# A gated product over rows: groups of four rows, two loads and one store a group, all on one DMA queue

## The chip, the core and the metric

The kernel runs on one core of a Trainium2 chip. The metric is the device time of one execution in microseconds (us). The engines that matter here are ScalarE (ACT), which computes the sigmoid, VectorE (DVE), which multiplies, SyncE (SP), which issues DMAs, and the core's 16 DMA engines, which move all data between memory (HBM) and the on-chip buffers of 128 partitions (SBUF). PE has no work, and GpSimd (POOL) only sets constants and clears semaphores.

## What is computed

```python
x = np.random.randn(8192, 8192).astype(np.float32)

def reference(x):
    a, b = np.split(x, 2, axis=-1)
    return a * (1 / (1 + np.exp(-b)))
```

Each row of x has 8192 numbers. The first half is multiplied by the sigmoid of the second half. 268.4 MB are read and 134.2 MB are written.

## The kernel before

**Tiles.** A tile is 256 rows: each of 128 partitions takes R = 2 adjacent rows, 64 KiB, which lie in one piece in memory. There are 32 tiles, `n_tiles`. The input buffers `xs` are two slots of 64 KiB a partition, and the output buffers `os` are two slots of 32 KiB a partition. Tile i uses slot i % 2 of both.

**One tile.** `load` (line 48) is one DMA of 8.4 MB on SP's queue, which appears in the profile as q1. `work` computes the sigmoid in place on ACT (line 61) and the product on DVE (line 72) into the packed output buffer. For most tiles this is one instruction of 128x8192 on each engine; the first and the last tile are worked in four pieces of 128x2048 (`fourths`). `store` (line 82) is one DMA of 4.2 MB, 32 KiB a partition, on ACT's queue, which appears as q10. Only the last tile is stored from SP's queue, in four parts of 1 MiB, each after its own product.

**What sets the order.** All waits are written by hand.
- A load waits at line 50 until the products of the tile two before it are done, because then its input slot is free. Loads 0 and 1 wait for nothing, and load 0 is moved ahead of the start-up barrier by `_launch_early`.
- The first sigmoid of a tile waits for its load (line 63).
- The first product of a tile waits on `ready` (line 65). This counts the sigmoid of this tile and the landing of the store two tiles earlier, which frees the output slot. Further pieces wait for their own sigmoid.
- A store waits for the products of its tile (line 83).

The queue of SP therefore holds the loads in order, and ACT's instruction stream alternates between a sigmoid and the issue of a store. `close` waits for everything and resets the semaphores.

Of the kernel before, what the change touches and what calls it, by code (L numbers as in the profile page):

```python
# [1 line left out]

# [4 lines left out]

P = 128
R = 2
SLOTS = 2  # L10


class _Program:

    def __init__(self, nc, x, out):
        self.nc = nc
        fp32 = mybir.dt.float32
        n_rows, n_cols = x.shape
        self.half = n_cols // 2  # L30
        self.n_tiles = n_rows // (P * R)
        self.x = x.rearrange("(n p r) m -> n p (r m)", p=P, r=R)
        self.out = out.rearrange("(n p r) m -> n p (r m)", p=P, r=R)
        self.xs = [nc.alloc_sbuf_tensor(f"x_sb{s}", [P, R * n_cols], fp32).ap() for s in range(SLOTS)]
        self.os = [nc.alloc_sbuf_tensor(f"o_sb{s}", [P, R * self.half], fp32).ap() for s in range(SLOTS)]
        self.loaded = [nc.alloc_semaphore(f"loaded{s}") for s in range(SLOTS)]
        self.ready = [nc.alloc_semaphore(f"ready{s}") for s in range(SLOTS)]
        self.product = nc.alloc_semaphore("product")
        self.sigmoid = nc.alloc_semaphore("sigmoid")
        self.arrived = nc.alloc_semaphore("arrived")  # L40
        self.last = nc.alloc_semaphore("last")
        self.to_ready = [0] * SLOTS
        self.products = self.sigmoids = self.lasts = 0
        self.done = {}

    def load(self, i, after=None):
        s = i % SLOTS
        ins = self.nc.sync.dma_start(out=self.xs[s][:, :], in_=self.x[i]).then_inc(self.loaded[s], 16)
        if i >= SLOTS:
            ins._wait_ge(self.product, self.done[i - SLOTS])  # L50
        return ins

    def work(self, i, pieces):

        nc, s = self.nc, i % SLOTS
        rows = self.xs[s].rearrange("p (r h m) -> p r h m", r=R, h=2)
        packed = self.os[s].rearrange("p (r m) -> p r m", r=R)
        waits = []
        for k, (r, c) in enumerate(pieces):
            b = rows[:, r, 1, c]  # L60
            sig = nc.scalar.activation(out=b, in_=b, func=mybir.ActivationFunctionType.Sigmoid)  # L61
            if k == 0:
                sig._wait_ge(self.loaded[s], 16 * (i // SLOTS + 1))
                self.to_ready[s] += 1 + (16 if i >= SLOTS else 0)
                waits.append((self.ready[s], self.to_ready[s]))
                sig.then_inc(self.ready[s], 1)
            else:
                self.sigmoids += 1
                waits.append((self.sigmoid, self.sigmoids))
                sig.then_inc(self.sigmoid, 1)  # L70
        for (r, c), wait in zip(pieces, waits):
            mul = nc.vector.tensor_mul(out=packed[:, r, c], in0=rows[:, r, 0, c], in1=rows[:, r, 1, c])  # L72
            mul._wait_ge(*wait)
            mul.then_inc(self.product, 1)
            self.products += 1
        self.done[i] = self.products

    def store(self, i, lo=0, hi=None, products=None):
        s, final = i % SLOTS, i == self.n_tiles - 1
        hi = R * self.half if hi is None else hi  # L80
        queue = self.nc.sync if final else self.nc.scalar
        ins = queue.dma_start(out=self.out[i][:, lo:hi], in_=self.os[s][:, lo:hi])
        ins._wait_ge(self.product, self.done[i] if products is None else products)
        if final:
            self.lasts += 16
            ins.then_inc(self.last, 16)
        else:
            ins.then_inc(self.ready[s], 16)
        return ins

    def trace(self):

        n, half = self.n_tiles, self.half
        whole = [(slice(0, R), slice(0, half))]
        fourths = [(slice(r, r + 1), slice(h * half // 2, (h + 1) * half // 2)) for r in range(R) for h in range(2)]
        self.load(1)
        for i in range(n):
            self.work(i, fourths if i in (0, n - 1) else whole)
            if i + SLOTS < n:
                self.load(i + SLOTS)  # L100
            if i < n - 1:
                self.store(i)
        for k in range(4):
            self.store(n - 1, k * half // 2, (k + 1) * half // 2, self.products - 3 + k)

    def close(self):


        nc, s = self.nc, (self.n_tiles - 2) % SLOTS
        for engine in (nc.scalar, nc.vector, nc.sync):  # L110
            engine.drain().then_inc(self.arrived, 1)  # L111
        nc.gpsimd.wait_ge(self.arrived, 3)
        nc.gpsimd.wait_ge(self.ready[s], self.to_ready[s] + 16)
        ids = sorted(h.num for h in (*self.loaded, *self.ready, self.product, self.sigmoid, self.arrived))
        assert ids == list(range(ids[0], ids[-1] + 1)) and self.last.num not in ids
        nc.gpsimd.sem_clear(range(ids[0], ids[-1] + 1))
        nc.gpsimd.drain()
        nc.sync.wait_ge(self.last, self.lasts).then_inc(self.last, -self.lasts)


def _launch_early(nc):

    SP = mybir.EngineType.SP
    entry, body = (b.instructions for b in nc.main_func.blocks[:2])
    load = next(i for i in body if i.engine == SP and i.opcode == "DMACopy")
    assert not load.sync_info.on_wait
    body.remove(load)
    where = next(k for k, i in enumerate(entry) if i.engine == SP and i.opcode == "Drain")  # L130
    entry.insert(where, load)


@with_exitstack
def kernel(
    ctx: ExitStack,
    tc: tile.TileContext,
    x: bass.AP,
    out: bass.AP,
):  # L140
    nc = tc.nc
    prog = _Program(nc, x, out)
    tc.info.no_tile_sem_insts.add(prog.load(0).ins.name)
    tc.close()
    tc.compile()  # L145
    _launch_early(nc)
    prog.trace()
    prog.close()


# [1 line left out]
_INS = ['x']  # L152
_OUTS = [((8192, 4096), 'float32')]


# [23 lines left out]
```

## Time and profile before

| what | value |
|---|---|
| median of 3 runs | 933.23 us (933.12 to 933.39) |
| the profiled execution | 933.08 us |
| its span | 931.8 us |
| DVE busy | 278.6 us (30%), 38 instructions |
| ACT busy | 226.8 us (24%), 39 instructions |
| moved over the span | 402.67 MB, 432 GB/s |
| q1, SP's queue | 5184 packets, 272.63 MB |
| q10, ACT's queue | 4464 packets, 130.03 MB |
| load, issue to landing | 42.2 us (median of 32) |
| store on ACT's queue, issue to landing | 34.8 us (median of 31) |

The span is the profiled part of the execution; the rest of its 933.08 us lies around it. A DMA is split into packets, and here a packet is the piece of one partition: 64 KiB of a load, 32 KiB of a store, 8 KiB of one of the four last stores. Each transfer also ends with 16 small packets of 4 bytes, one on each DMA engine, which raise the semaphore that others wait for. The share of a queue is the time that its packets took, against 16 engines' span.

### The profile page before, as it was taken

How to read it: one execution, taken by the hardware profiler on the slowest of the kernel's cores; microseconds unless marked ns; L12 is line 12 of the kernel's file. 1: busy time of each engine (PE TensorE's matmuls, PEld its weight loads, DVE VectorE, ACT ScalarE, POOL GpSimd, SP SyncE). 2: the span in 40 equal slices, each digit the busy share in tenths (PEclk: the TensorE clock that was granted, in tenths of full speed). 3: DMA queues.
4: the chain of work that ended last, by engine and by line, in shares of the span. 5: the costliest groups of instructions: out<-in, count | busy, mean ns of one | idle time of the engine just before them, and what ended most of it. 6: DMA issues, size and time to landing. Idle time of an engine off the chain costs nothing.

```text
span 931.8 us, 190 instructions
## 1 busy us (share of the span) xinstructions
DVE 278.6 (30%) x38; ACT 226.8 (24%) x39; POOL 0.2 (0%) x4
## 2 busy tenths in 40 slices
DVE  0333213333133331233312333123331233312333
ACT  1323330233311333113331133311333203332033
POOL 0000000000000000000000000000000000000000
DMA  9999999999999999999999999999999999999999
GB/s 405 428 450 428 422 456 405 450 428 428 450 421 435 428 436 442 428 428 450 450 405 430 442 456 428 412 463 408 450 428 428 450 408 447 428 428 450 426 429 405
DMA packets 9649, 402.67 MB, mean 432 GB/s; under 512 B 1072, under 2 KB 1072, under 8 KB 1072
## 3 DMA queue, kind: packets, MB, share of 16 engines
q1 hardware_dynamic: 5184, 272.63, 67.7%
q10 hardware_dynamic: 4464, 130.03, 32.3%
q14 instruction: 1, 0.01, 0.0%
HBM read 268.44 MB, written 134.22 MB: 432 GB/s over the span
## 4 chain that ended last, share of the span: by engine, by line
DMA 73%; DVE 15%; ACT 12%; DVEq 0%; issue 0%
DMA x_sb<-in_x_dram 73%; DVE o_sb L72 15%; ACT x_sb L61 12%; DVEq L111 0%
## 5 line engine op out<-in xcount | busy, mean ns | idle before, releaser
L72 DVE TENSOR_TENSOR o_sb<-x_sb 128x8192 f32<-128x8192 f32 (+1 forms) x38 | 278.6, 7344 | 647.1 <-ACT x_sb L61 647.1
L61 ACT ACTIVATE x_sb<-x_sb 128x8192 f32<-128x8192 f32 (+1 forms) x38 | 225.5, 5949 | 693.9 <-DMA x_sb<-in_x_dram 693.9
L61 ACT ACT_TABLE_LOAD x1 | 1.3, 1283 | 1.4 <-PEq L145 1.4
L163 POOL MEMSET const-bfloat16-1.0<- 128x1 bf16 x1 | 0.1, 102 | 0.0
L163 POOL MEMSET const-uint8-127<- 128x1 uint8 x1 | 0.1, 102 | 0.0
L163 POOL MEMSET const-float32-0.0<- 128x1 f32 x1 | 0.1, 99 | 0.2 <-issue 0.2
L163 POOL MEMSET const-float32-1.0<- 128x1 f32 x1 | 0.1, 99 | 0.0
## 6 DMA issues: line engine op xcount, KB each, us to landing
out_dram<-o_sb ACTq DMA_DIRECT2D x31, 4096.0 KB, 34.8
out_dram<-o_sb SPq DMA_DIRECT2D x4, 1024.0 KB, 5.7
x_sb<-in_x_dram SPq DMA_DIRECT2D x32, 42.2
```

What stands on the lines that cost most here:

```text
L61: sig = nc.scalar.activation(out=b, in_=b, func=mybir.ActivationFunctionType.Sigmoid)
L72: mul = nc.vector.tensor_mul(out=packed[:, r, c], in0=rows[:, r, 0, c], in1=rows[:, r, 1, c])
L163: nc = _bacc.Bacc("TRN2", target_bir_lowering=False, num_devices=1)
```

## The change

Rows are now taken in groups of four for each partition, so that a group is 512 rows and there are 16 groups. A group is still loaded as two tiles of two rows each, into the two input slots. The tile of even number takes the first 64 KiB of each partition's 128 KiB, the odd one the second. There is now one output buffer of 64 KiB a partition, as large as the two were together. The products of the two tiles lie in it side by side, and one DMA stores the 64 KiB of every partition, 8.4 MB in all, after the odd tile. All DMAs are issued from SP, so ACT issues none.

The product of an even tile waits until the store of the group before has landed, since there is only one output buffer. Even tiles are worked as one piece of 128x8192, odd tiles and tile 0 as two pieces of 128x4096. The last group is stored in parts: the even tile's half at once, 32 KiB a partition, then the odd tile's as 8, 8 and 16 KiB a partition, after pieces of 128x2048, 128x2048 and 128x4096. On SP's queue the order is load 2g+2, store of group g, load 2g+3.

The core of the diff:

```diff
-        self.x = x.rearrange("(n p r) m -> n p (r m)", p=P, r=R)
-        self.out = out.rearrange("(n p r) m -> n p (r m)", p=P, r=R)
-        self.xs = [nc.alloc_sbuf_tensor(f"x_sb{s}", [P, R * n_cols], fp32).ap() for s in range(SLOTS)]
-        self.os = [nc.alloc_sbuf_tensor(f"o_sb{s}", [P, R * self.half], fp32).ap() for s in range(SLOTS)]
+        self.x = x.rearrange("(g p r) m -> g p (r m)", p=P, r=2 * R)
+        self.out = out.rearrange("(g p r) m -> g p (r m)", p=P, r=2 * R)
+        self.xs = [nc.alloc_sbuf_tensor(f"x_sb{s}", [P, self.tile], fp32).ap() for s in range(2)]
+        self.os = nc.alloc_sbuf_tensor("o_sb", [P, 2 * self.packed], fp32).ap()
...
+    def load(self, i):
+        g, s = divmod(i, 2)
+        part = self.x[g][:, s * self.tile : (s + 1) * self.tile]
+        ins = self.nc.sync.dma_start(out=self.xs[s], in_=part).then_inc(self.loaded[s], 16)
+        if i > 1:
+            ins._wait_ge(self.product, self.products)
...
             if k == 0:
-                sig._wait_ge(self.loaded[s], 16 * (i // SLOTS + 1))
-                self.to_ready[s] += 1 + (16 if i >= SLOTS else 0)
-                waits.append((self.ready[s], self.to_ready[s]))
-                sig.then_inc(self.ready[s], 1)
+                sig._wait_ge(self.loaded[s], 16 * (g + 1))
+            if k == 0 and s == 0:
+                self.to_ready += 1 + (16 if g else 0)
+                waits.append((self.ready, self.to_ready))
+                sig.then_inc(self.ready, 1)
...
+    def store(self, g, lo, hi, products, final=False):
+        ins = self.nc.sync.dma_start(out=self.out[g][:, lo:hi], in_=self.os[:, lo:hi])
+        ins._wait_ge(self.product, products)
...
+        whole = [(0, R, 0, half)]
+        by_row = [(r, r + 1, 0, half) for r in range(R)]
+        to_end = [(0, 1, 0, half // 2), (0, 1, half // 2, half), (1, 2, 0, half)]
         self.load(1)
         for i in range(n):
-            self.work(i, fourths if i in (0, n - 1) else whole)
-            if i + SLOTS < n:
-                self.load(i + SLOTS)
-            if i < n - 1:
-                self.store(i)
-        for k in range(4):
-            self.store(n - 1, k * half // 2, (k + 1) * half // 2, self.products - 3 + k)
+            g, s = divmod(i, 2)
+            self.work(i, to_end if i == n - 1 else by_row if s or i == 0 else whole)
+            if i < n - 2:
+                if s:
+                    self.store(g, 0, 2 * packed, self.products)
+                self.load(i + 2)
+            elif i == n - 2:
+                self.store(g, 0, packed, self.products, final=True)
+            else:
+                done = self.products - len(to_end)
+                for k, (r0, r1, c0, c1) in enumerate(to_end):
+                    lo = packed + r0 * half + c0
+                    self.store(g, lo, lo + c1 - c0, done + k + 1, final=True)
```

In `close` the wait for the store before the last one (line 113) is gone.

## The prediction

> **What bounds the kernel now.** I read the page from its second part to its fifth, then the chain in order of time, then busy time by stage, and last the single DMA packets recorded in the trace (a start, a length in ns and a size for each). DVE is busy 30% of the span and ACT 24%, so neither can be the bound. The DMA lines of the page:
>
> ```profile
> DMA  9999999999999999999999999999999999999999
> ...
> q1 hardware_dynamic: 5184, 272.63, 67.7%
> q10 hardware_dynamic: 4464, 130.03, 32.3%
> ```
>
> The two queues' packets fill 67.7 + 32.3 = 100.0% of 16 engines' span: q1 is SP's (loads and the last four stores), q10 is ACT's (31 stores). The chain of waits says something else at first sight; one round of it:
>
> ```profile
> 60.54 42.07 DMA x_sb<-in_x_dram
> 102.61 0.02 issue
> 102.64 7.04 ACT x_sb L61
> 109.67 0.02 issue
> 109.70 8.70 DVE o_sb L72
> 118.40 0.02 issue
> 118.42 42.30 DMA x_sb<-in_x_dram
> ```
>
> It reads load, sigmoid, multiply, next load, as if 15.7 us of computing (7.04 + 8.70) stood in every round of 58 us. But two slots run such chains half a round apart, and the DMA engines do not stop while one of them computes. Busy time by stage shows it (columns: window, its length, DVE, ACT, POOL busy, clock, DMA share, GB/s); first loads alone, then a round, then all other rounds, then the end:
>
> ```profile
> 4.36:31.00 26.64, 7.27 (x4) 7.31 (x4) 0.00 (x0) 1.00 1.00 435
> 60.54:118.42 57.88, 17.38 (x2) 14.06 (x2) 0.00 (x0) 1.00 1.00 435
> 118.42:872.69 754.27, 226.00 (x26) 182.76 (x26) 0.00 (x0) 1.00 1.00 434
> ```
> ```profile
> 924.00:926.00 2.00, 1.66 (x1) 0.00 (x0) 0.00 (x0) 1.00 1.01 426
> 926.00:928.00 2.00, 0.00 (x0) 0.00 (x0) 0.00 (x0) 1.00 1.02 430
> ```
>
> Loads alone, loads with stores, and stores alone (the two lines from 924 us on) all run at a share of about 1.00. So the time is a sum of packet times, and the change is worth what it does to that sum, plus whatever gaps it opens.
>
> **The price list, from the packet records.** On one engine a 64 KiB packet starts 2.4148 us after the one before (mean of the first load), a 32 KiB one takes 1.2095 (stores between stores), an 8 KiB one 0.3064 (last stores). That is a line: about 301.2 ns per 8 KiB and 5 ns per packet. By recorded length (2418, 1213, 309 ns) the fixed part is 8 ns. A semaphore write ending a transfer costs about 3 ns: a steady tile repeats every 29.00 us, and 8 x 2.4148 + 8 x 1.2095 = 28.99. Two stretches stand out: the very first packets (some 3.1 us, 0.7 over) and the load packet ahead of the first store (3.35 us, 0.95 over, at 35.8 us on all engines). A later one of 0.24 us, at 762 us, is alone.
>
> **The change, term by term** (per engine, so each term is time of the span).
>
> 1. Stores by size. Before: 31 x 8 of 32 KiB and 4 x 8 of 8 KiB, 248 x 1.2095 + 32 x 0.3064 = 309.76 us. After: 15 x 8 of 64 KiB, 8 of 32, 16 of 8, and 8 of 16 KiB (not in the trace; 0.61 from the line): 289.78 + 9.68 + 4.90 + 4.86 = 309.22. So -0.54; by recorded lengths -1.0. I take -0.55, since spacings are what adds up, and keep -1.0 for the range. Store packets of 64 KiB are not in the trace either; load packets of that size are the nearest row. The loads keep their number and size: 0.
> 2. Sixteen semaphore writes fewer (67 transfers become 51): 16 x 3 ns = -0.05.
> 3. ACT's queue is not used any more. The 0.95 us stretch came when q10 got its first work. The other stretch is the first use of q1, by a load; when q1 had run dry and got work again at 919 us, no packet was stretched. That fits "first use of a queue" better than "first store", so I take -0.95; if it belongs to the first store it stays, so 0 to -0.95.
> 4. ACT issues 31 stores less, at 0.36 us; ACT was idle 694 us waiting for loads, so 0. SP issues 15 more, at 0.33 us each; it waits 861 us for products at the loads' line: 0.
> 5. One queue keeps its order. It holds, for group g: load 2g+2, store g, load 2g+3. An engine runs dry if the next item is issued too late. Durations, from the groups by shape:
>
> ```profile
> L72 DVE TENSOR_TENSOR o_sb<-x_sb 128x8192 f32<-128x8192 f32 x30 | 260.8, 8692 | 608.3 <-ACT x_sb L61 608.3
> L61 ACT ACTIVATE x_sb<-x_sb 128x8192 f32<-128x8192 f32 x30 | 210.9, 7029 | 653.0 <-DMA x_sb<-in_x_dram 653.0
> L72 DVE TENSOR_TENSOR o_sb<-x_sb 128x2048 f32<-128x2048 f32 x8 | 17.8, 2286 | 38.8 <-ACT x_sb L61 38.8
> L61 ACT ACTIVATE x_sb<-x_sb 128x2048 f32<-128x2048 f32 x8 | 14.6, 1898 | 41.0 <-DMA x_sb<-in_x_dram 41.0
> ```
>
> The new 128x4096 pieces lie between: sigmoid 1.90 to 7.03, product 2.29 to 8.69; on the straight lines 3.61 and 4.42. Each of the three transfers takes 8 x 2.4148 = 19.3 us. Let load 2g end on the first engine at 0; the last is 0.5 us later. Store g-1 runs to 19.3, load 2g+1 to 38.6, load 2g+2 to 57.95. There is one output buffer, so the product of tile 2g waits for store g-1 to land: 19.9 + 8.7 = 28.6 releases load 2g+2, 10 us ahead of 38.6. Tile 2g+1 starts at 39.2: + 3.6 + 2 x 4.4 = 51.7 releases store g, 6.3 us ahead of 57.95. On SP only load 2g+3 stands behind it, due at the same moment. How much lead an issue needs, the trace bounds: 1.37 us for load 0 on idle engines, 2.17 at 919.08 (first packet 921.25), and 6.5 to 7.6 from a store's issue to its first packet while another queue's work is in hand. [...] So 0; if 7.6 were needed, 1.3 us per group. In the beginning, tile 0 in halves is done at 21.8 + 3.6 + 8.8 = 34.2, and load 1 ends at 40.6: 0.
> 6. The end. After load 31 lands (A), half of store 15 (9.7 us, queued long before) and two 8 KiB pieces (4.9) keep the first engine busy until A + 14.1. The pieces are released at A + 4.4 and 6.6. The last one, 128x4096, needs two sigmoids of 1.9, one of 3.6 and 4.4: released at A + 11.9, a lead of 2.2. That just covers 2.17: 0, and a few tenths if not. The last store is now twice as large, but it costs its bytes alone, which are in term 1: at load 31's landing 8.4 MB are left to store, where it was 17.1 us x 434 GB/s = 7.4.
>
> Sum: -0.55 - 0.05 - 0.95 = -1.55. Against the profiled execution's 933.08 us (a span of 931.8 and 1.3 around it): 931.5. The median of the runs shown is 0.15 higher, 933.23, so **931.7 us**. A measurement of this kernel can tell about 0.2%, 1.87 us, from no change; the line lies at 931.4, and the forecast is on its near side: the same, by a hair's breadth under faster.
>
> [...] The first two loads stood in one queue; on every engine the second's packet starts 2 ns after the 9 ns semaphore write of the first (21.27 us). [...]
>
> **The rivals.**
> - *A stall where the ring turns from loads to stores* (slower). No boundary of that kind inside one ring is in the trace. Its place is the head of each group store, its price at most the 0.95 us of term 3: 15 x 0.95 = 14, so 946 us (961 if the turn back costs as much); with the small stretch of 0.24 us at each, 935.3. It decides from 3.4/15 = 0.23 us per group on. Against it: before, every engine turns from a load packet to a store packet and back each 3.62 us, some 250 times, with nothing between; but there two rings take turns. Chance 0.11.
> - *The store comes late* (slower): lead 7.6 needed, 15 x 1.3 + 5.4 at the end = 25, 957 us. For it only the longest of three rows. 0.05.
> - *The wider pitch slows packets* (slower). A load now takes 64 KiB of every 128 KiB, where it was one run. Each 1% on 376 packets is 9 us: 941. Against it: the last stores take 8 KiB of every 32 KiB and lie on the same line as the rest. 0.05. [...]
> - *Stores are still cut at 32 KiB*, so the change gives no larger packets: only terms 2 and 3, 932.2. 0.05.
>
> **How the numbers follow.** Forecast 0.74, alone 930.9 to 932.8 (term 1 at -1.0; term 3 at 0). Below 931.4 needs the recorded lengths or another tenth: 0.20 of the 0.74. Same: 0.54 + 0.05 = 0.59. Slower: 0.11 + 0.05 + 0.05 = 0.21. The range, 930.8 to 935.5, takes in the mild stall at 935.3 and leaves the rest of the slower cases out.
>
> **What would show it.** Right: one data queue of about 100%, no packet gap after 2 us, some 58.0 us from group to group, DVE waiting about 12 us per group for the store's landing, store packets of about 2418 ns, and no packet over 3 us after the first. Wrong: stretched packets at each store's head, a DMA share under 1.00 in the middle windows, load packets longer than 2418, or a hole ahead of the last store.

## The result, and the profile after

The changed kernel takes 938.10 us (median of 6 runs, 936.04 to 939.02), against 933.33 us for the kernel before in the same session (6 runs). The ratio is 1.0047, with an interval of 1.0034 to 1.0060: slower by half a per cent, where 931.7 us was forecast. The profiled execution took 938.71 us, of which 937.3 are its span.

The page of the changed kernel, its DMA lines:

```profile
DMA  9999999999999999999999999999999999999997
...
q1 hardware_dynamic: 7344, 402.66, 99.6%
...
L77 DVE TENSOR_TENSOR o_sb<-x_sb 128x4096 f32<-128x4096 f32 (+2 forms) x50 | 279.5, 5618 | 650.0 <-DMA out_dram<-o_sb 399.5
```

One queue carries everything, with fewer packets (7344 where there were 9648), and DVE waits for the group store, 15 times. So the change does what it says. The engines are still busy nearly all the time; only the last slice shows a 7. A packet that takes longer counts as busy, so the share of busy time can't show where 5.5 us of span went.

The chain of waits can. It passes once through every group: store issued, load behind it landed, sigmoid, two products, next store. These are its DMA steps (start, length, what), from the issue behind a group store to the landing of load 2g+3:

```profile
54.22 46.06 DMA x_sb<-in_x_dram
...
113.13 45.85 DMA x_sb<-in_x_dram
...
171.83 45.91 DMA x_sb<-in_x_dram
...
347.82 45.13 DMA x_sb<-in_x_dram
...
405.79 45.15 DMA x_sb<-in_x_dram
...
638.33 45.70 DMA x_sb<-in_x_dram
...
871.20 46.61 DMA x_sb<-in_x_dram
```

Some rounds take 45.13 us, and their groups follow each other by 57.97 us, which is the forecast of 58.0. Others take up to 1.5 us more. Over all 15 rounds (seven are shown) the lengths above 45.13 add up to 6.8 us. 930.2 us of span forecast + 6.8 = 937.0, against 937.3 measured. So the arithmetic of the forecast holds, and one thing is missing in it.

The packet records show where it sits. They have no engine number, but each packet starts where the one before it on its engine ended (to within 0.02 us, up to 921 us), and so they can be sorted into 16 chains. The table counts what 64 KiB load packets took beyond 2418 ns, at the last packet of a load that stands ahead of a store, as a mean over the 16 engines; "at" is the packet's start, and "spread" is the time between the first and the last engine there:

```
changed kernel, last load packet ahead of a store, all 16 turns
at us        58    116   174   233   291   349   407   465   523   581   639   697   755   814   872   911
mean, us     0.86  0.13  0.43  0.25  0.10  0.03  0.05  0.10  0.16  0.01  0.12  0.02  0.15  0.08  0.16  0.61
spread, us   0.8   0.7   1.5   2.0   2.8   3.2   3.2   3.2   3.8   3.8   3.8   4.4   4.4   4.5   4.7   5.5
```

All other 64 KiB packets after the first together cost under 0.5 us on 13 engines and 0.8 to 1.1 on three. So the packets stall where the queue turns from loads to stores. On the slowest engine these packets lost 6.3 us over the kernel, on the fastest 1.3, in the mean 3.3. The stall drives the engines apart (from 0.8 us at the first turn to 5.5 at the last), and the last engine decides when a load has landed: load 31's last writes came at 911.8 us on the first engine and at 917.5 on the last, and it had landed at 917.8. About half of what the chain lost is the mean stretch, the rest is that it did not fall evenly. The end shows it too (window, length, DVE, ACT, POOL busy, clock, DMA share, GB/s); the changed kernel:

```profile
914.00:922.00 8.00, 2.23 (x2) 4.17 (x3) 0.00 (x0) 1.00 0.92 393
922.00:930.00 8.00, 6.69 (x3) 3.05 (x1) 0.00 (x0) 1.00 0.75 313
930.00:938.80 8.80, 0.00 (x0) 0.00 (x0) 0.00 (x0) 1.00 0.59 248
```

and the kernel before:

```profile
914.00:922.00 8.00, 5.24 (x3) 7.18 (x4) 0.00 (x0) 1.00 0.92 397
922.00:930.00 8.00, 3.66 (x2) 0.13 (x1) 0.00 (x0) 1.00 1.01 426
930.00:938.80 8.80, 0.00 (x0) 0.00 (x0) 0.00 (x0) 1.00 0.10 41
```

From 921 us on, with the DMA share at 0.75 and 0.59, early engines of the changed kernel stand idle while the late ones work off what they have left.

### The profile page after: what moved, and what is told of

Read it like the earlier page. It is cut to its first block, busy times and chain, and to the rows that moved or that the text cites. A ratio compares the mean times of both kernels' runs of the same rounds, so it can differ in the third digit from the quotient of the medians.

```text
span 937.3 us, 197 instructions
## 1 busy us (share of the span) xinstructions
DVE 279.5 (30%) x50; ACT 227.9 (24%) x51; POOL 0.2 (0%) x4
## 2 busy tenths in 40 slices
DMA packets 7344, 402.66 MB, mean 430 GB/s; under 512 B 816, under 2 KB 816, under 8 KB 816
## 3 DMA queue, kind: packets, MB, share of 16 engines
q1 hardware_dynamic: 7344, 402.66, 99.6%
## 4 chain that ended last, share of the span: by engine, by line
DMA 77%; DVE 15%; ACT 6%; SPq 1%; ACTq 0%; issue 0%
DMA x_sb<-in_x_dram 77%; DVE o_sb L77 15%; ACT x_sb L65 6%; SPq L85 1%; ACTq L118 0%
## 5 line engine op out<-in xcount | busy, mean ns | idle before, releaser
L77 DVE TENSOR_TENSOR o_sb<-x_sb 128x4096 f32<-128x4096 f32 (+2 forms) x50 | 279.5, 5618 | 650.0 <-DMA out_dram<-o_sb 399.5
L65 ACT ACTIVATE x_sb<-x_sb 128x4096 f32<-128x4096 f32 (+2 forms) x50 | 226.6, 4566 | 695.7 <-DMA x_sb<-in_x_dram 695.7
## 6 DMA issues: line engine op xcount, KB each, us to landing
out_dram<-o_sb SPq DMA_DIRECT2D x15, 26.6
```

The costliest lines, as they stand in the source:

```text
L77: mul = nc.vector.tensor_mul(out=packed[:, r0:r1, c0:c1], in0=rows[:, r0:r1, 0, c0:c1], in1=rows[:, r0:r1, 1, c0:c1])
```

## The experiments

Ratios are against the kernel before, run on the same chip in turns.

**e1: the queue alone.**

```diff
-        queue = self.nc.sync if final else self.nc.scalar
+        queue = self.nc.sync
```

> The kernel before with one change: all its stores go on SP's queue. Theory A (a turn from loads to stores inside one ring stalls the DMA engines as long as they turn in step): 31 turns, the last load packet ahead of a store stretched by about 0.9 us at first and less as the engines drift apart; the engines end some us apart, time 936 to 943 us. Theory B (what costs is the new layout: rows in fours, store packets of 64 KiB): this kernel has neither, so 932.5 to 933.5 us and no stretch but the one at the first store.

937.96 us, ratio 1.0048 (1.0035 to 1.0060). That is as much as the whole change loses, from one line. Its page:

```profile
q1 hardware_dynamic: 9648, 402.66, 99.7%
```

The packets are those of before in number and size. The last load packets lose 0.82 us at the first turn and less than 0.2 in the mean at each later one; nothing is left after 700 us. Eleven engines lose 0.8 to 1.3 us in all, the slowest 4.9. Theory A holds so far, though 31 turns cost no more than the 16 of the changed kernel: the price is not so much a turn.

**e2: rows of four alone.**

```diff
-        self.x = x.rearrange("(n p r) m -> n p (r m)", p=P, r=R)
-        self.out = out.rearrange("(n p r) m -> n p (r m)", p=P, r=R)
+        xg = x.rearrange("(g p t r) m -> g t p (r m)", p=P, t=2, r=R)
+        self.x = [xg[i // 2, i % 2] for i in range(self.n_tiles)]
+        og = out.rearrange("(g p t r) m -> g t p (r m)", p=P, t=2, r=R)
+        self.out = [og[i // 2, i % 2] for i in range(self.n_tiles)]
```

> The kernel before with one change: rows are taken in fours, so that a load's 64 KiB pieces lie 128 KiB apart and a store's 32 KiB pieces 64 KiB apart; queues, slots and sizes as before. Theory A: 933.3 us, as before, within 0.3 us. Theory B (the layout costs): 936 us or more, packets longer than 2418 and 1213 ns.

933.16 us, ratio 0.9998 (0.9989 to 1.0007). The wider pitch costs nothing, and theory B falls for the layout.

**e3: the group stores on ACT's queue.**

```diff
-        ins = self.nc.sync.dma_start(out=self.out[g][:, lo:hi], in_=self.os[:, lo:hi])
+        queue = self.nc.sync if final else self.nc.scalar
+        ins = queue.dma_start(out=self.out[g][:, lo:hi], in_=self.os[:, lo:hi])
```

> The changed kernel with its group stores on ACT's queue. A store of 8.4 MB now shares the engines with the loads and takes some 39 us, and with one output buffer the next product comes late: some 2 us of idle engines a group, 950 to 965 us. What is looked at is the packet ahead of each store. Theory A (turn inside one ring): no stretch except at the first store, as before. Theory C (any start of stores after loads alone, whichever ring): a stretch of some 0.9 us at the head of all 15 stores.

1013.87 us, ratio 1.0858 (1.0844 to 1.0873): more than any theory said. The idle time per group had been put too low. The waits of e3 (who waited for what: us in total, times, longest):

```profile
DVE o_sb L77 <- DMA out_dram<-o_sb: 654.1, 15, 44.3
```

A store needs 43.5 us (median) beside the loads, and the next product waits for it with the only output buffer. What counts here is the head of each store. There every engine's load packet is stretched, by 1.0 to 1.3 us in the mean, at all 15 stores, and again by 0.5 to 0.8 where loads start on idle engines. So theory A was too narrow: it is not the one ring. A store that starts beside loads alone costs the stall on two rings too. In the kernel before, the queue of stores never runs empty after 39 us: the next store is issued 5.7 us before the last one has landed (60.55 and 66.25), and no later store pays: from 40 us on its load packets took 2421 ns at most, but for one of 2659 ns at 762 us. And here, where the waits bring the engines back together each time (spread 0.6 us), the price does not fall from store to store.

**e4: no computing.** The diff of the wait; `work` is gone, and one memset fills the output buffer:

```diff
-            ins._wait_ge(self.product, self.products)
+            ins._wait_ge(self.loaded[s], 16 * g)
...
+        self.nc.vector.memset(self.os, 0.0).then_inc(self.product, 1)
...
-                    self.store(g, 0, 2 * packed, self.products)
+                    self.store(g, 0, 2 * packed, (self.loaded[1], 16 * (g + 1)) if g else (self.product, 1))
```

> The changed kernel without sigmoid and products: the output buffer is set to zero once and stored for every group, loads wait for the load two before to land, a store for its second tile to land. The same transfers in the same order on one ring, nothing on ACT, next to nothing on DVE, and issues at least as early. Theory A: the last load packet ahead of a store is stretched as in the changed kernel, 0.9 us at the first turn; the slowest engine loses 3 to 8 us, 934 to 939 us. Theory D (late issues, or DVE and ACT in the way of the transfers): no stretch, about 930 to 931 us.

938.98 us, ratio 1.0057 (1.0043 to 1.0070). Its page:

```profile
DVE 13.7 (1%) x1; POOL 0.2 (0%) x4
...
q1 hardware_dynamic: 7344, 402.66, 99.6%
```

With no work on ACT and one instruction on DVE the stretches are there, 1.13 us at the first turn and up to 6.6 over all turns on the slowest engine. Theory D falls: neither the compute engines nor late issues make them. Two things must be added. The last four stores of e4 wait until load 31 has landed, and every engine stands idle ahead of them, 5.6 us on the earliest and 1.2 on the latest; so some 1.2 us of its time are not of the turns. And four later turns (near 408, 582, 641 and 815 us) still cost 0.4 to 0.7 us in the mean, with the engines 2.6 to 3.6 us apart.

**e5: engines out of step.**

```diff
+        for k, lo, hi in ((8, 0, 2 * packed), (4, 0, packed), (2, packed, packed + half)):
+            at = 8 if k < 8 else 0
+            ins = self.nc.sync.dma_start(out=self.os[at : at + k, lo:hi], in_=self.x[0][at : at + k, lo:hi])
+            ins.then_inc(self.ready, 16)
+            self.to_ready += 16
         self.load(1)
```

> The changed kernel with three small extra loads into the output buffer ahead of load 1, on 8, 4 and 2 of the 16 DMA engines, so that two engines run 4.2 us late, two 3.6, four 2.4 and eight on time. Theory C2 (the stall at a turn comes from engines that turn at the same moment): the first turn costs less than half of the changed kernel's 0.86 us a packet in the mean, and the later ones less too; the end is set by the late engines, some 934 to 937 us in spite of 4.2 us of extra work on two engines. Rival (each engine pays for its own turns, in step or not): 0.86 us stays, and 940 to 943 us.

956.16 us, ratio 1.0239 (1.0226 to 1.0252): a miss, in the first place of the experiment itself. The extra packets of 64 KiB went to eight partitions side by side. All 16 packets of 64 KiB that the engines had in hand then, the eight extra ones among them, took 7.9 to 9.2 us, where 2.4 was meant. No packet was stretched at the first turn, but 0.2 to 0.5 us in the mean were lost at many later ones, at turns back to loads too. e11 repeats it cleanly.

**e6: the end of before.**

```diff
-        to_end = [(0, 1, 0, half // 2), (0, 1, half // 2, half), (1, 2, 0, half)]
+        to_end = [(r, r + 1, h * half // 2, (h + 1) * half // 2) for r in range(R) for h in range(2)]
```

> The changed kernel with its last tile in four pieces of 128x2048 and four stores of 1 MiB, as before, so that the last store is released about 1 us earlier and is half as large. If the slowest engine sets the end, which never waits there: as the changed kernel, 936 to 939 us. If the holes of 2.4 us that the other engines show ahead of the last store cost time: 2 to 3 us less, 933.5 to 936.

939.19 us, ratio 1.0058 (1.0046 to 1.0071), just above the 936 to 939 of the first reading. The holes in front of the last store are gone from the early engines (0.2 to 1.1 us are left ahead of the first 1 MiB part) and nothing is won.

**e7: stores of a group in packets of 32 KiB.** Rows are dealt out as before, and the store of a group has two runs a partition:

```diff
-        self.x = x.rearrange("(g p r) m -> g p (r m)", p=P, r=2 * R)
-        self.out = out.rearrange("(g p r) m -> g p (r m)", p=P, r=2 * R)
+        self.x = x.rearrange("(n p r) m -> n p (r m)", p=P, r=R)
+        self.out = out.rearrange("(g t p r) m -> g p t (r m)", p=P, t=2, r=R)
...
-        part = self.x[g][:, s * self.tile : (s + 1) * self.tile]
+        part = self.x[i]
...
+            ins = self.nc.sync.dma_start(out=self.out[g], in_=self.os.rearrange("p (t m) -> p t m", t=2))
...
```

> The changed kernel with the rows dealt out as before: a load's 128 pieces lie one behind the other again, and the one store of a group consists of 256 packets of 32 KiB instead of 128 of 64 KiB. Theory C2: the same turns at the same places, 936 to 940 us, 0.86 us stretch at the first. If 64 KiB store packets or the group's layout cost the time: about 933.

939.34 us, ratio 1.0066 (1.0054 to 1.0078), first turn 1.19 us, slowest engine 6.8. The size of the store packets is not the cause.

**e8: loads and stores in quarters of the partitions.**

```diff
...
+        for k in range(4):
+            p = slice(k * P // 4, (k + 1) * P // 4)
+            ins = self.nc.sync.dma_start(out=self.xs[s][p, :], in_=self.x[i][p]).then_inc(self.loaded[s], 16)
             ins._wait_ge(self.product, self.done[i - SLOTS])
-        return ins
+            self.part(i - SLOTS, p)
...
```

> The kernel before with all DMAs on SP's queue, but from tile 2 on each load and the store of the tile two before cut into four by partitions and issued in turns: every engine gets 2 load packets, 2 store packets, and so on, in one ring, four times as many turns as with whole tiles (some 120). If every turn in a ring costs while the engines are in step: stretches at most of the early turns, 936 to 945 us. If only a run of loads alone longer than a few packets fills what then has to drain, or the stores only have to be always at hand: no stretch after the first store, 933 to 934 us (256 more small transfers at some ns each).

1391 us in the profiled execution, 1530 to 1546 in the five others. Nothing on turns can be read from this. The page's row of GB/s in 40 slices:

```profile
GB/s 423 283 270 287 264 286 275 295 308 284 296 288 277 308 280 301 294 279 301 289 280 304 283 282 295 282 283 288 290 284 294 285 289 294 292 295 301 271 288 225
```

It falls from 423 to some 290 as soon as transfers of 32 partitions begin. The extra loads of e5, to eight partitions side by side, were slow too (7.9 to 9.2 us a packet). What makes them slow was not shown. e10 cuts by columns instead.

**e9: the same transfers with one turn.** From e4:

```diff
             if i < n - 2:
-                if s:
-                    self.store(g, 0, 2 * packed, (self.loaded[1], 16 * (g + 1)) if g else (self.product, 1))
                 self.load(i + 2)
+        for g in range(n // 2 - 1):
+            self.store(g, 0, 2 * packed, (self.landed[g % 2], 16 * (g // 2)) if g > 1 else (self.product, 1))
...
```

> The kernel without sigmoid and products again (e4), the same transfers on the same one queue, but all 32 loads first and then all stores of zeros: one turn from loads to stores instead of 16. If the turns are what the one queue costs: one stretch of 0.9 to 1.2 us, all other packets at 2418 ns, a span of 931 to 932 us, time 932 to 933.5 us. If one queue, or store packets of 64 KiB, cost by themselves: 938 us as e4.

932.24 us, ratio 0.9989 (0.9981 to 0.9998). Its page:

```profile
span 931.6 us, 98 instructions
...
q1 hardware_dynamic: 7344, 402.66, 100.0%
```

The same packets on the same single queue as e4 take 6.7 us less (932.24 and 938.98, each against the same time of before within 0.01), and the 0.4% of idle time is gone. Some 1.2 us of the 6.7 are e4's wait ahead of its last stores; the other 5.5 or so go with the repeated turns. One queue and 64 KiB store packets cost nothing by themselves: 932.24 us is 0.9989 of the kernel before. The spread stays at 0.45 us to the end. One detail was missed: at the only turn, at 622 us, no packet is stretched. Instead the load packets between 38 and 73 us lost 0.81 us an engine in all, up to 0.17 us each, with no store in sight.

**e10: sixty turns.** From e4, with loads and stores in quarters by columns:

```diff
...
+                for k in range(2):
+                    self.quarter(i + 2, 2 * k)
+                    self.quarter(i + 2, 2 * k + 1)
+                    m = 2 * i + k
+                    self.store(m // 4, m % 4 * packed // 2, (m % 4 + 1) * packed // 2, (self.product, 1))
...
```

> e4 with every load from tile 2 on and every group store cut into quarters by columns, over all 128 partitions, in the order load, load, store: 60 turns, a run of loads alone of 9.7 us instead of 38.7. The packets of 16 KiB cost 1080 x 5.3 ns = 5.7 us more and the semaphore writes 0.4, so 937.6 us without any turn. If a turn costs some 0.9 us each time: 990 us. If, as in e1, the cost fades with the engines' drift and ends at 5 to 7 us for the slowest engine however many turns there are: 941 to 946. If a short run of loads costs nothing at its end: 937 to 938.5.

942.45 us, ratio 1.0096 (1.0082 to 1.0110): 4.9 us above the 937.6 worked out without turns. The slowest engine lost 4.2 us in stretched packets. The time is the second case's: nearly four times the turns of the changed kernel cost no more than its 16 do. That drift is the reason, as the second case has it, is not shown by this.

**e11: out of step, cleanly.** As e5, but the extra loads go to every fourth partition:

```diff
+        for k, first, lo, hi in ((8, 0, 0, 2 * packed), (4, 32, 0, packed), (2, 32, packed, packed + half)):
+            rows = slice(first, first + 4 * k, 4)
+            ins = self.nc.sync.dma_start(out=self.os[rows, lo:hi], in_=self.x[0][rows, lo:hi])
...
```

> [...] Two engines 4.2 us late, two 3.6, four 2.4, eight on time. Theory C2 (a turn costs what the engines that turn together make it cost): no or half a stretch at the first turn; 930.2 + 4.2 + 1.3 = 935.7 us if later turns cost next to nothing either. If engines apart still stretch packets at later turns, as e5's trace shows (6.9 us in the mean over all turns): 939 to 943.

942.48 us, ratio 1.0096 (1.0080 to 1.0111). The extra packets now took 2.42, 1.21 and 0.61 us as planned, and theory C2 falls. At the first turn the eight engines in time, in step within 0.5 us, lost some 0.03 us each. The eight late ones lost 0.85 to 1.5 us each on theirs. So turning together is not enough to pay, and here those pay that are still loading when others have begun to store. At later turns the other traces lean the same way: the eight engines that came last to each turn bear 31.0 of 38.5 us summed over all engines in the changed kernel, over 90% in e1 and 70% in e4. The first turn of the changed kernel does not fit: the engine that came there first, when none had begun to store, lost 1.23 us, the most of all. In e11 turns back from stores to loads cost too, up to 0.4 us in the mean.

## Why the prediction was wrong

Two terms of the sum failed. The head of each group store was put at nothing, and term 3 took 0.95 us off that did not go. In their place stretched packets came at the 16 turns, 6.3 us on the slowest engine, and the chain of waits lost 6.8 us, 0.9 of them in the first round and 5.9 in the fourteen others. The first rival, "a stall where the ring turns from loads to stores", had the place and the decisive point right (0.23 us a group; 0.45 a round came), and no turn of the changed kernel passed its 0.95 us in the mean, but it was given a chance of 0.11. Its mechanism, the one ring, was not right either: in e3 stores on the other ring pay as well, and in e9 the one ring turns once without any cost. Two readings led there:

- *"Every engine turns from a load packet to a store packet and back each 3.62 us ... with nothing between."* That is true, and it says nothing of this change. Taking turns between two queues that both have work is not the same as starting stores after loads alone. e3 showed that the start of a store beside loads costs on two rings too; e9 and e4 that the repeated starts make the difference.
- *Term 3*: the 0.95 us stretch ahead of the first store was taken for the first use of q10 and counted as saved. In the changed kernel q10 is unused, and 0.86 us stand at the first turn all the same; in e1, with one queue too, 0.82. It was the one specimen of such a stretch that the trace held, and it was read as a reason for the forecast. Whether it belongs to the store is open, since in e9 loads alone lose as much (0.81 us an engine).

The other steps, by their own numbers:

1. Stores by size, -0.55: not seen alone, but a group without a stretch takes 57.97 us, as the price list has it, and the whole sum closes to 0.3 us. The 64 KiB store packets took 2418 ns.
2. Right: between transfers the next packet follows as closely as it did between the first two loads, 6 ns (median) after the start of the 4-byte write in both kernels.
3. Failed, see above.
4. Right: nothing seen on ACT or SP.
5. Right: on no engine is there a gap between packets before 921 us. That a lead of 2.2 us is enough on the one queue, and not 7.6, was the author's choice, and nothing before the change showed it. In the changed kernel the first packet of a group store came 6.7 us after its issue on the earliest engine at the first turn and 1.85 us after it at the fifteenth, still without a gap. The wait that DVE shows for the group store, 26.6 us a time, looks larger than the 12 that were announced because it also holds the time before the sigmoid.
6. Half right. The last store was issued at 929.5 us, and its first packet came at 930.4. Ten engines stood idle for 2.2 to 2.6 us before it, more than "a few tenths", because the term kept the 0.5 us between the first and the last engine, and it had grown to 5.5. The slowest engines had no gap at all, so it cost nothing, and e6 won nothing by removing it.

Some of its numbers were off without bearing on the outcome. Times of packets stand 0.37 us later in the prediction than in the trace, where load 0's first packet starts 1.01 us after its issue, not 1.37; lengths and gaps are right, and the leads are shorter by as much. Of the long leads, the trace of the kernel before shows that two more load packets start on each engine between the issue of the first store (32.66 us) and its first packet (38.8 to 39.3); why was not shown. The 961 us of the first rival is 960 by its own terms, and 930.9, the lower end of the forecast, is 931.2.

The rival of the wider pitch was priced too high at any price: e2 gives 0.9998. Late stores did not happen. The range ended at 935.5, with a mild stall of 0.24 us a group; 0.45 was inside the rival's own bounds and outside the range.

Which engine issues the stores was not without a price here: e1 differs from the kernel before in the issuing engine of 31 stores alone, and its ratio is 1.0048.

No version that computes beats the kernel before by more than these runs can tell. Packets that take 100% of the span leave about 1 us (e9, without computing, ran at 0.9989).

## What to carry to other kernels

When the DMA engines are busy all the time, look at single packets, not at busy shares: a stretched packet counts as busy (the queue's share is 99.6% in the changed kernel), and a loss of half a per cent sat in 16 places. Of the orders tried here with computing, two queues that both always have work were the fastest (933.33 us, against medians of 937.96 us or more on one queue). A store that started after a run of loads alone cost up to 1.3 us in the mean (e3), though not always (nothing at the one turn of e9), and after the first turn mostly on the engines that were late already, so that the landing, which waits for the last engine, moved further than the mean (6.8 us against 3.3 in the changed kernel). A single odd stretch in a trace is the first specimen of something, and a change that multiplies its circumstances should be priced with it.

## What the runs showed of the hardware

- The loss at a turn falls on the last load packet ahead of a store, and after the first turn mostly on late engines. From 0.86 us at the first turn of the changed kernel it drops to 0.01 to 0.43 at the later ones, with 0.61 at the last; in e1 nothing is left after 700 us (spread 4.7 us). In e3, where the engines are brought back into step (spread 0.6 us), it does not drop (1.0 to 1.3 us at all 15 stores). But distance between the engines does not protect by itself: e4 has turns of 0.4 to 0.7 us with engines 2.6 to 3.6 us apart, and in e11, with engines 4 us apart from the beginning, 0.1 to 0.4 us remained at many turns. In the kernels on one queue whose engines started in step, the slowest engine lost 4.2 to 6.8 us in stretched packets, whether there were 16, 31 or 60 turns. What sets this sum, and what in the engines or behind them stalls, was not found.
- Nor was it found why the only turn of e9, at 622 us, costs nothing, while its loads alone lose 0.81 us an engine between 38 and 73 us. The first-turn price of the other kernels is of the same size (0.86 us at 58 us in the changed kernel) and falls in the same stretch of time, so part of it may not belong to the turn. The loss at later turns is untouched by this.
- In e9, 64 KiB load packets start 2.417 us apart in a long run of loads, store packets 2.414: both directions run at some 434 GB/s alone, and the kernel before has 434 with both mixed.
- Transfers over 32 adjacent partitions brought the rate from 423 to some 290 GB/s (e8).
